# A decoder layer on one core: FFN weights staged earlier, gate blocks in single PSUM banks, two low halves moved to GpSimd

## The chip, the cores and the metric

The kernel runs on one core of a Trainium2 chip. Its time is device microseconds (us). Before the change it took 1652.49 us, the median of three runs (1648.84 to 1655.51). The profiled execution, from which all rows below come, took 1650.32 us; its span, from the first to the last instruction, is 1648.2 us. Engines: PE is TensorE (PEld its weight loads), DVE VectorE, ACT ScalarE, POOL GpSimd, SP SyncE; SPq, DVEq and so on are their queues.

## What is computed

One decoder layer on x of 1024 tokens by 1024 channels, in float32. The change touches its FFN only:

```python
    for i in range(DEPTH):
        h = rms_norm(x, g_mix[i])
        ...
        x = x + merged @ w_out[i]
        hf = rms_norm(x, g_ffn[i])
        x = x + (jax.nn.silu(hf @ w_ffn_gate[i]) * (hf @ w_ffn_up[i])) @ w_ffn_down[i]
        hp = rms_norm(x, g_ple[i])
        x = x + jax.nn.sigmoid(hp @ w_ple_gate[i]) * (p[i] @ w_ple_proj[i])
```

D_FF is 2816, so the gate and the up matrix have 22 blocks of 128 columns each.

## The kernel before

**Numbers and products.** Activations lie transposed, 128 channels by 1024 tokens per tile; a half of the tokens (512) is a column of PSUM work. Every float32 operand is split into a high and a low part (`split_w`, `split_x`: ACT copies the high part, L143 and L178; DVE or POOL subtracts, L144 and L179, to get the low part), and `gemm` (L181) adds three matmuls per piece of 128: high by high, high by low, low by high.

**Weights.** `want` writes a plan of all weights in the order of their use; `load(n)` issues the DMAs of the first n of the plan into two `raw` buffers, `stage(n)` splits the first n of the plan into high and low tiles, and `weights(name, i)` (L164) hands out the next one: it stages up to two ahead of the running number `weights.at`, loads three ahead, and then counts `weights.at` up. Both lists only grow, so `stage(n)` with an n below what is staged already does nothing.

**The FFN's front.** Inside a stretch whose order is the program's own (`tc.manual_schedule()`), eight blocks of w_out add into x (`out_block`), then the first two gate and up blocks, f = 0 and 1 (`FIRST`), are computed as plain products by `gate_up` (L1109), four calls: blocks 0 and 1 on the first half of the tokens, then blocks 0 and 1 on the second half. A call makes the gate product into PSUM, applies Silu on ACT (L1123) into a tile `sil`, makes the up product into PSUM, multiplies on DVE (L1127), and stores the hidden block. The list `between` holds work put into a call: after five eighths of the gate product, after the Silu, and after the multiplication. In the first call these are the statistics of the second half's norm (`nf[1].stats(1)`: a column sum on PE, L212, a scale on DVE, L203, and a power on POOL, L205) and the norm of that half (`later_half`: L1064 on DVE, then a split of each of eight units). The weights of block 1 are kept in tiles named `wk`, since both halves use them.

**PSUM.** Products go to `PG` tiles (two banks, two buffers) or `PM` tiles (one bank, three buffers); the column sums and the norms' replicated scales are `PM` tiles. An instruction that fills a buffer waits for the readers of what stood in it.

**Strassen pairs.** The other 20 gate and up blocks go in pairs through one level of Strassen's scheme (`strassen`, L1165): seven products of sums of weights (`pair_make`, from two raw tiles) and sums of activations (`sum_units`, L1073: DVE forms a sum, L1080, ACT its high half, DVE or POOL its low half, L179). The first pair's products run in the order 2, 4, 5, 3, 1, 6, 7; products 2 and 5 share one `PG` tile, 4 and 3 another; `six_seven(0)` and `six_seven(2)` make the eight sums for products 6 and 7 between products 4 and 5 and between 5 and 3. After them come the second pair's `pair_make` and its products. Outside the manual stretches a list scheduler sets the order.

**Into the down product.** A second manual stretch holds the last pair's products, the reload of the first hidden blocks (`hidden_load`, tiles `hd`, `fah`, `fal`), and `down` (L1277), whose weights `w_fd` come next in the plan. Ahead of the last pair's products stand two calls, `stage(1)` and `load(2)`.

Of the kernel before, what the change touches and what calls it, by code (L numbers as in the profile page):

```python
# [56 lines left out]
FIRST = (0, 1)  # L57
# [14 lines left out]
def tile_layer(ctx: ExitStack, tc: tile.TileContext, A, out):  # L72
    nc = tc.nc
    pe, dve, act, pool, sp = nc.tensor, nc.vector, nc.scalar, nc.gpsimd, nc.sync
# [10 lines left out]
    def nm(s):  # L85
        cnt[0] += 1
        return f"{s}_{cnt[0]}"

    def U(name="u", dt=F32, shape=(P, S)):
        return up.tile(list(shape), dt, tag="u", name=nm(name))  # L90
# [9 lines left out]
    def PG():  # L100
        return gp.tile([P, S], F32, tag="g", name=nm("g"))

    def PM(shape=(P, 512)):
        return mp.tile(list(shape), F32, tag="m", name=nm("m"))
# [14 lines left out]
    def pump(gen, k=1):  # L119
        for _ in range(k):  # L120
            next(gen, None)
# [12 lines left out]
    def load_w(src):  # L134
        n = src.shape[-1]
        raw = UW("raw", F32)[:, :n]
        sp.dma_start(raw, src)
        return raw

    def split_w(raw, lo_eng, keep):  # L140
        n = raw.shape[-1]
        hi, lo = (U("wk", FR), U("wk", FR)) if keep else (UW("whi")[:, :n], UW("wlo")[:, :n])
        act.activation(hi, raw, AF.Copy)  # L143
        lo_eng.tensor_tensor(lo, raw, hi.bitcast(F32), op=ALU.subtract)  # L144
        return hi, lo
# [8 lines left out]
    def load(n):  # L154
        while len(loaded) < min(n, len(plan)):
            n_, i_ = plan[len(loaded)][:2]
            loaded.append(load_w(A[n_] if i_ is None else A[n_][i_]))

    def stage(n):
        while len(made) < min(n, len(plan)):  # L160
            load(len(made) + 1)
            made.append(split_w(loaded[len(made)], *plan[len(made)][2:]))

    def weights(name, i=None, ahead=2):  # L164

        at_ = weights.at
        assert plan[at_][:2] == (name, i), (plan[at_], name, i)
        stage(at_ + ahead)
        load(at_ + ahead + 1)
        weights.at += 1  # L170
        t = made[at_]
        made[at_] = None
        return t
# [7 lines left out]
    def gemm(groups, W, X, k0=0, k1=None, fill=None, per=()):  # L181


        K = len(W)
        for k in range(k0, K if k1 is None else k1):
            if fill is not None:
                pump(fill, per[k])
            for t, (wi, xi) in enumerate(((0, 0), (0, 1), (1, 0))):
                for ps, sl in groups:
                    pe.matmul(ps, lhsT=W[k][wi], rhs=X[k][xi][:, sl],  # L190
                              start=(k == 0 and t == 0), stop=(k == K - 1 and t == 2))
# [4 lines left out]
    def wk(wt, K, off=0, width=P, stride=P):  # L196
        return [(wt[0][:, off + k * stride: off + k * stride + width],
                 wt[1][:, off + k * stride: off + k * stride + width]) for k in range(K)]
# [75 lines left out]
    xs = []  # L274
# [726 lines left out]
    for n2 in range(4):  # L1001
        wt = weights("w_ao", n2)
        for i in range(2):
# [4 lines left out]
            ps = PG()  # L1008
# [33 lines left out]
    XS, B12, B21 = {}, [], []  # L1042
# [4 lines left out]
    def x_unit(dst, a, lo_eng=None):  # L1047

        u = U("xc", FR)
        split_x(*parts(u), a, lo_eng)  # L1050
        dst.append(parts(u))

    def xs(i):
        return XS.setdefault(i, [])

    def norm_half(hf, r):

        sl = HV[hf]
        rep = replicate(r, 4)[0]
        yield  # L1060
        for k in range(9):
            if k < 8:
                h = x2[k][:, sl]
                dve.scalar_tensor_tensor(h, h, vec(V_FFN + k), rep, op0=ALU.mult, op1=ALU.mult)  # L1064
            if k:
                x_unit((B12 if k < 5 else xs(5)) if hf else (xs(2) if k < 5 else B21), x2[k - 1][:, sl])
            yield
# [5 lines left out]
    def sum_units(*iks, lo_eng=None):  # L1073
        todo = []
        for j, (i, k) in enumerate(iks):
            (p, u), op, (q, v) = SUMS[i]
            if j % 2 == 0:
                t = U("xsum")
            a = t[:, HV[j % 2]]
            dve.tensor_tensor(a, x2[p + k][:, HV[u]], x2[q + k][:, HV[v]], op=op)  # L1080
            todo.append((xs(i), a))
        for dst, a in todo:
            x_unit(dst, a, lo_eng)

    nf = [Norm(V_FFN) for _ in range(2)]

    def out_block(n, hf, before=None):
        wt = weights("w_out", n)
        pump(before or iter(()), 2)
        ps = PG()  # L1090
        gemm([(ps[:, 0:512], HV[hf])], wk(wt, 8), mT)
        dve.tensor_tensor(x2[n][:, HV[hf]], x2[n][:, HV[hf]], ps[:, 0:512], op=ALU.add)
        nf[hf].square(n, HV[hf])
        sp.dma_start(spill_x[n][:, HV[hf]], x2[n][:, HV[hf]])
# [7 lines left out]
    def hidden(f, s, sl):  # L1102
        if f not in spill_h:
            spill_h[f] = dp.tile([P, S], F32, tag=f"hd{f}", name=nm("hd"))
        sp.dma_start(spill_h[f][:, sl], s[:, sl])
# [3 lines left out]
    def gate_up(f, s, hf, X, between=()):  # L1109


        sl, half = HV[hf], slice(0, 512)
        between = [b or (lambda: None) for b in between] + [lambda: None] * (3 - len(between))
        for name in ("w_fg", "w_fu"):
            if (name, f) not in firsts:
                firsts[name, f] = weights(name, f)
            wt = firsts[name, f]
            ps = PG()
            if name == "w_fg":
                gemm([(ps[:, half], half)], wk(wt, 8), X, 0, 5)  # L1120
                between[0]()
                gemm([(ps[:, half], half)], wk(wt, 8), X, 5)
                act.activation(s[:, sl], ps[:, half], AF.Silu)  # L1123
                between[1]()
            else:
                gemm([(ps[:, half], half)], wk(wt, 8), X)
                dve.tensor_tensor(s[:, sl], s[:, sl], ps[:, half], op=ALU.mult)  # L1127
                hidden(f, s, sl)
                between[2]()
# [3 lines left out]
    def pair_load(m):  # L1133

        name, i = m
        ra, rb = UW("raw", F32), UW("raw", F32)
        for t, c, j in ((ra, 0, 0), (ra, 1, 1), (rb, 0, 1), (rb, 1, 0)):
            sp.dma_start(t[:, HV[c]], A[name][i + c][:, HV[j]])
        raws[m] = ra, rb
# [79 lines left out]
    with tc.manual_schedule():  # L1219
        nh = None  # L1220
        for n in range(8):
            out_block(n, 1, nh)
            if n == 0:
                nf[0].stats(0)
            if n == 1:
                nh = norm_half(0, nf[0].r)
                pump(nh)
        pump(nh, 9)
        hs = [U("sil") for _ in FIRST]
        one_of = lambda i, lo_eng=None: lambda: sum_units(*((i, k) for k in range(4)), lo_eng=lo_eng)  # L1230

        def later_half():
            pump(norm_half(1, nf[1].r), 99)

        def pair0():
            pair_load(ms[0])
            one_of(4, pool)()

        def pair1():
            pair_load(ms[1])  # L1240

        def six_seven(k):
            return lambda: (sum_units((6, k), (7, k)), sum_units((6, k + 1)), sum_units((7, k + 1), lo_eng=pool))

        gate_up(FIRST[0], hs[0], 0, xs(2) + B21, (lambda: nf[1].stats(1), later_half))
        gate_up(FIRST[1], hs[1], 0, xs(2) + B21, (None, None, pair0))
        gate_up(FIRST[0], hs[0], 1, B12 + xs(5), (None, one_of(3), lambda: pair_make(ms[0])))
        gate_up(FIRST[1], hs[1], 1, B12 + xs(5), (None, one_of(1), pair1))
        gated(ms[0], strassen(ms[0], {4: six_seven(0), 5: six_seven(2), 1: lambda: pair_make(ms[1], pool)}))
# [5 lines left out]
    def hidden_load(ci, fs=None):  # L1255
        for f in fs or CHUNKS[ci]:
            h, hi, lo = U("hd"), U("fah", FR), U("fal", FR)
            sp.dma_start(h, spill_h[f])
            split_x(hi, lo, h)
            aa.setdefault(ci, []).append((hi, lo))  # L1260
# [34 lines left out]
    with tc.manual_schedule():  # L1295
        def back(*fs):
            return lambda: hidden_load(0, fs)

        stage(1)
        load(2)  # L1300
        rr = strassen(ms[-1], {4: back(*CHUNKS[0][:2]), 5: back(*CHUNKS[0][2:])})
        for n in range(2):
            x2_load(n)
        gated(ms[-1], rr)
        for ci in range(len(CHUNKS) - 1):
            nxt = load_next(ci, (2, 3, 5, 6))
            for n in down(ci, (0, 1), nxt):
                if ci == 0 and n < 6:
                    x2_load(n + 2)
# [14 lines left out]
    for hf in range(2):  # L1324
        sl = HV[hf]
        for n in range(8):
# [3 lines left out]
            ps, s, o = PG(), U("psig"), U("o")  # L1330
# [79 lines left out]
```

## Time and profile before

| | |
|---|---|
| median of three runs | 1652.49 us (1648.84 to 1655.51) |
| profiled execution: time, span | 1650.32 us, 1648.2 us |
| PE, DVE, ACT, POOL busy, share of the span | 97%, 69%, 43%, 9% |
| mean granted TensorE clock | 0.987 of full speed |
| chain that ended last | PE 51%, DVE 3%, ACT 1% of the span in merged steps |
| hand-over w_out to FFN, first blocks | about 854 to 935 us of the span |
| last pair to down product | about 1267 to 1316 us of the span |

How to read it: PE works nearly without a break, so what counts is each stretch in which it stands still, what ended that stretch, and how fast its next matmuls go. Busy time of other engines counts where PE waits for them. In a timeline a row is a run of like instructions: start, length, engine, line, operation, tiles, count, and in brackets the engine's idle time before it and what ended that.

### The profile page before, as it was taken

How to read it: one execution, taken by the hardware profiler on the slowest of the kernel's cores; microseconds unless marked ns; L12 is line 12 of the kernel's file. 1: busy time of each engine (PE TensorE's matmuls, PEld its weight loads, DVE VectorE, ACT ScalarE, POOL GpSimd, SP SyncE). 2: the span in 40 equal slices, each digit the busy share in tenths (PEclk: the TensorE clock that was granted, in tenths of full speed). 3: DMA queues.
4: the chain of work that ended last, by engine and by line, in shares of the span. 5: the costliest groups of instructions: out<-in, count | busy, mean ns of one | idle time of the engine just before them, and what ended most of it. 6: DMA issues, size and time to landing. Idle time of an engine off the chain costs nothing.

```text
span 1648.2 us, 20331 instructions
## 1 busy us (share of the span) xinstructions
PE 1592.8 (97%) x7736; PEld 1328.4 (81%) x7736; DVE 1139.4 (69%) x1806; ACT 714.5 (43%) x1066; POOL 147.0 (9%) x134
## 2 busy tenths in 40 slices
PE   7999999999999999999998899999999799999998
PEld 5888888888878888878886678888888688888887
DVE  4669999884899777656476766777766444446763
ACT  5456475868733677633243332232233222113441
POOL 2100100000202421320001100000000000000210
PEclk9999999999999999999999999999999899999999
DMA  7430122222222854246441122222221542223263
GB/s 264 115 90 27 64 89 90 91 101 77 98 82 94 213 154 109 97 176 246 146 136 45 58 90 90 77 77 77 102 92 63 184 148 102 103 83 108 84 205 134
DMA packets 61538, 184.69 MB, mean 112 GB/s; under 512 B 7296, under 2 KB 7808, under 8 KB 61440
## 3 DMA queue, kind: packets, MB, share of 16 engines
q1 hardware_dynamic: 61440, 183.38, 32.9%
q8 instruction: 61, 1.00, 0.3%
q14 instruction: 37, 0.30, 0.1%
HBM read 134.60 MB, written 45.09 MB: 109 GB/s over the span
## 4 chain that ended last, share of the span: by engine, by line
PE 51%; DVE 3%; ACT 1%; issue 0%; DMA 0%; SPq 0%; ACTq 0%; DVEq 0%
PE g L190 41%; PE m L190 9%; DVE xsum L1080 1%; DVE xc L179 1%; DMA raw<-w_fd 0%; DVE x L1064 0%; ACT xc L178 0%; DVE wlo L179 0%; PE m L212 0%; PE f L190 0%; DVE h L248 0%; DVE raw L1157 0%; DVE c L1215 0%; ACT whi L178 0%; DVE sil L1127 0%
## 5 line engine op out<-in xcount | busy, mean ns | idle before, releaser
L143 ACT ACTIVATE whi<-raw 128x1024 fp32r<-128x1024 f32 x110 | 115.5, 1052 | 219.9 <-PE g L190 185.1
L190 PE MATMUL g<-hhi,whi 128*128 128x512 f32 (+2 forms) x656 | 200.9, 387 | 2.1 <-ACT vt L658 1.5
L190 PE MATMUL g<-hlo,whi 128*128 128x512 f32 (+2 forms) x656 | 199.4, 385 | 2.6 <-POOL hlo L179 1.3
L190 PE MATMUL g<-hhi,wlo 128*128 128x512 f32 (+2 forms) x656 | 199.4, 385 | 0.0
L144 DVE TENSOR_TENSOR wlo<-raw,whi 128x1024 fp32r<-128x1024 f32 x102 | 127.3, 1250 | 52.1 <-ACT whi L143 51.9
L613 DVE SCALAR_TENSOR_TENSOR cacc<-glu,vecs,cacc 128x994 f32<-128x994 f32 (+14 forms) x120 | 151.8, 1265 | 2.7 <-ACT cacc L610 1.9
L511 ACT ACTIVATE junka<-Y,tr 128x1024 bf16<-128x1024 f32 (+3 forms) x128 | 126.3, 987 | 46.0 <-DVE tr L536 23.2
L190 PEld LDWEIGHTS g<-hlo,whi 128*128 128x128 f32 (+1 forms) x656 | 122.1, 187 | 27.9 <-POOL hlo L179 2.1
L190 PEld LDWEIGHTS g<-hhi,whi 128*128 128x128 f32 (+1 forms) x656 | 121.6, 187 | 25.6 <-ACT vt L658 1.9
L190 PEld LDWEIGHTS g<-hhi,wlo 128*128 128x128 f32 (+1 forms) x656 | 122.1, 187 | 24.2
L1288 DVE TENSOR_TENSOR x<-x,g 128x1024 f32<-128x1024 f32 (+1 forms) x56 | 59.8, 1067 | 114.8 <-PE g L190 114.8
L205 POOL TENSOR_TENSOR r<-ms,mhalf 128x16 f32<-128x16 f32 (+2 forms) x14 | 34.8, 2489 | 1045.9 <-DVE ms L203 1030.3
L190 PE MATMUL g<-fah,whi 128*128 128x512 f32 x352 | 115.3, 394 | 9.8 <-ACT whi L143 9.4
L190 PE MATMUL g<-xc,whi 128*128 128x512 f32 x384 | 119.9, 393 | 4.7 <-DVE sil L1127 3.3
L190 PE MATMUL g<-fal,whi 128*128 128x512 f32 x352 | 114.5, 392 | 0.0
L190 PE MATMUL g<-fah,wlo 128*128 128x512 f32 x352 | 114.4, 392 | 0.0
L190 PE MATMUL g<-xc,w 128*128 128x512 f32 x480 | 112.0, 389 | 1.1 <-ACT w L178 1.1
L190 PEld LDWEIGHTS g<-xc,w 128*128 128x128 f32 x480 | 90.0, 188 | 20.2 <-ACT w L178 1.5
L190 PE MATMUL m<-xc,whi 128*128 128x512 f32 x320 | 99.1, 390 | 0.8 <-ACT xc L178 0.6
L190 PEld LDWEIGHTS g<-xc,whi 128*128 128x128 f32 x384 | 72.5, 190 | 20.7 <-DVE sil L1127 3.7
L190 PEld LDWEIGHTS g<-fah,whi 128*128 128x128 f32 x352 | 66.8, 190 | 24.7 <-ACT whi L143 9.9
L190 PEld LDWEIGHTS g<-fah,wlo 128*128 128x128 f32 x352 | 66.6, 189 | 14.1
(238 smaller groups left out, 3197.3 us busy)
## 6 DMA issues: line engine op xcount, KB each, us to landing
raw<-w_fd SPq DMA_DIRECT2D x26, 512.0 KB, 3.5
hd<-hd SPq DMA_DIRECT2D x22, 512.0 KB, 4.5
raw<-w_fg SPq DMA_DIRECT2D x40, 256.0 KB, 2.8
raw<-w_fu SPq DMA_DIRECT2D x40, 256.0 KB, 2.8
hd<-c SPq DMA_DIRECT2D x20, 512.0 KB, 2.8
x<-xT SPq DMA_DIRECT2D x16, 512.0 KB, 9.3
sgd<-sg SPq DMA_DIRECT2D x16, 512.0 KB, 2.9
raw<-w_out SPq DMA_DIRECT2D x16, 512.0 KB, 3.7
```

Of the source, the lines that this page charges most:

```text
L143: act.activation(hi, raw, AF.Copy)
L144: lo_eng.tensor_tensor(lo, raw, hi.bitcast(F32), op=ALU.subtract)
L179: (lo_eng or dve).tensor_tensor(lo, x, hi.bitcast(F32), op=ALU.subtract)
L190: pe.matmul(ps, lhsT=W[k][wi], rhs=X[k][xi][:, sl], start=(k == 0 and t == 0), stop=(k == K - 1 and t == 2))
L205: pool.tensor_tensor(r, ms, mhalf[:, :width], op=ALU.pow)
L511: act.activation(junka[:, :n], ysl(b), AF.Sign, scale=-1.0, bias=self.tr[:, c], accum_out=self.cn[:, c])
L613: dve.scalar_tensor_tensor(acc[:, sl], g, w, acc[:, sl], op0=ALU.mult, op1=ALU.add)
L1080: dve.tensor_tensor(a, x2[p + k][:, HV[u]], x2[q + k][:, HV[v]], op=op)
L1288: dve.tensor_tensor(x2[n][:, sl], x2[n][:, sl], ps[:, sl], op=ALU.add)
```

## The change

`gate_up` takes a `PM` tile for the gate product and keeps a `PG` tile for the up product. A function `first_stats` replaces the bare statistics in the first call and stages three ahead of the running number behind them. `six_seven` pairs the sums of one product in a tile instead of one sum of each, and gives both low halves of product 7 to POOL. `stage(1)` and `load(2)` become calls by the running number.

```diff
-            ps = PG()
+            ps = PM() if name == "w_fg" else PG()
...
+        def first_stats():
+            nf[1].stats(1)
+            stage(weights.at + 3)
+
...
         def six_seven(k):
-            return lambda: (sum_units((6, k), (7, k)), sum_units((6, k + 1)), sum_units((7, k + 1), lo_eng=pool))
-
-        gate_up(FIRST[0], hs[0], 0, xs(2) + B21, (lambda: nf[1].stats(1), later_half))
+            return lambda: (sum_units((6, k), (6, k + 1)), sum_units((7, k), (7, k + 1), lo_eng=pool))
+
+        gate_up(FIRST[0], hs[0], 0, xs(2) + B21, (first_stats, later_half))
...
-        stage(1)
-        load(2)
+        stage(weights.at + 1)
+        load(weights.at + 2)
         rr = strassen(ms[-1], {4: back(*CHUNKS[0][:2]), 5: back(*CHUNKS[0][2:])})
```

On ACT, at the first `gate_up` call, the order was (whi is the up weight of block 0, wk the two weights of block 1, xc the units of the second half's norm):

```order
L143 ACTIVATE whi_7779<-raw_7745 128x1024
L1123 ACT_TABLE_LOAD
L1123 ACTIVATE sil_7777<-g_7785 128x512
L178 ACTIVATE xc_7827<-x_1238_7131 128x512
...
L178 ACTIVATE xc_7854<-x_1252_7152 128x512
L143 ACTIVATE wk_7857<-raw_7783 128x1024
L143 ACTIVATE wk_7891<-raw_7861 128x1024
L1123 ACTIVATE sil_7778<-g_7895 128x512
```

and is now:

```order
L143 ACTIVATE whi_7779<-raw_7745 128x1024
L143 ACTIVATE wk_7810<-raw_7783 128x1024
L143 ACTIVATE wk_7816<-raw_7814 128x1024
L1123 ACT_TABLE_LOAD
L1123 ACTIVATE sil_7777<-m_7785 128x512
L178 ACTIVATE xc_7837<-x_1238_7131 128x512
...
L178 ACTIVATE xc_7864<-x_1252_7152 128x512
L1123 ACTIVATE sil_7778<-m_7895 128x512
```

The two `wk` copies moved from behind the norm's eight units to ahead of the first Silu; on DVE their low halves moved in the same way, from behind the eight units to right behind the statistics.

On SP, ahead of the last pair's products, the order was (raw from w_fd is the down product's weight, hd the reloaded hidden blocks and the stored ones):

```order
L1105 DMA hd_10551<-c_1736_10314 128x1024
L1258 DMA hd_10713<-hd_7889 128x1024
...
L1264 DMA x_1801_10810<-x2d_7136 128x1024
L1105 DMA hd_10813<-c_1774_10578 128x1024
L1105 DMA hd_10816<-c_1773_10577 128x1024
L137 DMA raw_10818<-w_fd 128x1024
L137 DMA raw_10824<-w_fd 128x1024
```

and is now:

```order
L1105 DMA hd_10549<-c_1734_10312 128x1024
L137 DMA raw_10680<-w_fd 128x1024
L137 DMA raw_10686<-w_fd 128x1024
L1262 DMA hd_10719<-hd_7893 128x1024
...
L1268 DMA x_1803_10816<-x2d_7136 128x1024
L1105 DMA hd_10819<-c_1772_10576 128x1024
L1105 DMA hd_10822<-c_1771_10575 128x1024
```

Two loads of w_fd moved ahead of four reloads of hidden blocks, two of x and two stores. The first one's high half now stands on ACT between the last weight copy of the last pair (L178) and the copy of product 5 of the pair before (L1185); its low half on DVE ahead of L1188.

On DVE, in the sums for products 6 and 7, the first half of the order was:

```order
L1182 TENSOR_TENSOR c_1410_8143<-s_1408_8141,g_8145 128x512
L1080 TENSOR_TENSOR xsum_8172<-x_1238_7131 128x512
L1080 TENSOR_TENSOR xsum_8172<-x_1246_7143 128x512
L179 TENSOR_TENSOR xc_8175<-xsum_8172,xc_8175 128x512
L179 TENSOR_TENSOR xc_8178<-xsum_8172,xc_8178 128x512
L1080 TENSOR_TENSOR xsum_8181<-x_1240_7134 128x512
L179 TENSOR_TENSOR xc_8183<-xsum_8181,xc_8183 128x512
L1080 TENSOR_TENSOR xsum_8186<-x_1248_7146 128x512
```

and is now:

```order
L1182 TENSOR_TENSOR c_1410_8143<-s_1408_8141,g_8145 128x512
L1080 TENSOR_TENSOR xsum_8172<-x_1238_7131 128x512
L1080 TENSOR_TENSOR xsum_8172<-x_1240_7134 128x512
L179 TENSOR_TENSOR xc_8175<-xsum_8172,xc_8175 128x512
L179 TENSOR_TENSOR xc_8178<-xsum_8172,xc_8178 128x512
L1080 TENSOR_TENSOR xsum_8181<-x_1246_7143 128x512
L1080 TENSOR_TENSOR xsum_8181<-x_1248_7146 128x512
```

One of three low halves left DVE, and the same in the second call; POOL has four in place of two. PE's order is the same but for the PSUM tiles' names.

## Rows read from the trace of the kernel before

**Rows 1.** The page's first part: busy time of each engine, its share of the span and its instructions.

```profile
PE 1592.8 (97%) x7736; PEld 1328.4 (81%) x7736; DVE 1139.4 (69%) x1806; ACT 714.5 (43%) x1066; POOL 147.0 (9%) x134
```

**Rows 2.** Who waited for whom, PE alone, over the whole span: what it waited for, us in total, times, the longest in us.

```profile
PE g L190 <- ACT whi L143: 9.4, 1, 9.4
...
PE g L190 <- ACT wk L143: 5.3, 1, 5.3
PE g L190 <- DVE sil L1127: 3.3, 1, 3.3
...
PE m L190 <- ACT one L178: 2.7, 1, 2.7
...
PE g L190 <- ACT w L178: 1.1, 1, 1.1
```

**Rows 3.** Busy time by stretch: us, then busy us and count of PE, PEld, DVE, ACT and POOL, the granted TensorE clock as a share of full speed, the DMA share and GB/s.

```profile
871.70:876.00 4.30, 4.24 (x11) 2.91 (x12) 2.96 (x3) 0.92 (x1) 0.00 (x0) 0.58 0.16 61
...
912.50:916.50 4.00, 3.98 (x10) 3.12 (x11) 0.00 (x0) 0.00 (x0) 0.00 (x0) 0.57 0.70 205
...
1309.80:1315.80 6.00, 5.93 (x14) 4.66 (x15) 2.45 (x2) 1.07 (x2) 0.00 (x0) 0.52 0.56 206
1316.00:1328.00 12.00, 12.00 (x54) 9.89 (x54) 4.71 (x4) 4.01 (x4) 0.00 (x0) 1.00 0.60 243
```

**Rows 4.** PE's timeline: the products of block 1 on the first half and on the second half of the tokens, and the first matmuls of the down product.

```profile
871.73 13.05 PE L190 MATMUL g<-xc,wk 128*128 128x512 f32 x48 [5.31 <-ACT wk L143]
...
895.49 11.04 PE L190 MATMUL g<-xc,wk 128*128 128x512 f32 x48
...
1309.87 1.22 PE L190 MATMUL g<-fah,whi 128*128 128x512 f32 x2 [9.44 <-ACT whi L143]
```

**Rows 5.** The timelines of ACT, DVE and SP in the FFN's front, 853 to 885 us.

```profile
860.53 0.60 ACT L1123 ACTIVATE sil<-g 128x512 f32<-128x512 f32 x1 [2.78 <-PE g L190]
...
870.63 1.99 ACT L143 ACTIVATE wk<-raw 128x1024 fp32r<-128x1024 f32 x2
...
860.97 1.41 DVE L1064 SCALAR_TENSOR_TENSOR x<-x,vecs,m 128x512 f32<-128x512 f32 x2 [2.48 <-PE m L222]
...
869.99 1.47 DVE L179 TENSOR_TENSOR xc<-x,xc 128x512 fp32r<-128x512 f32 x2
...
884.88 0.69 DVE L1127 TENSOR_TENSOR sil<-sil,g 128x512 f32<-128x512 f32 x1 [10.21 <-PE g L190]
...
855.27 0.38 SPq L137 DMA_DIRECT2D raw<-w_fg  x1
857.73 0.33 SPq L137 DMA_DIRECT2D raw<-w_fu  x1
```

**Rows 6.** DMA issues of whole weight blocks: count, KB each, median us from issue to landing; and the smallest, median and largest time to landing of the four w_fd loads between 1265 and 1325 us.

```profile
raw<-w_fg SPq DMA_DIRECT2D x2, 512.0 KB, 3.4
raw<-w_fu SPq DMA_DIRECT2D x2, 512.0 KB, 3.9
...
DMA to landing us min/median/max: 3.6/5.3/7.9
```

**Rows 7.** The timelines of SP, DVE and ACT from the pair before the last to the down product, 1267 to 1312 us.

```profile
1278.17 9.02 SPq L1258 DMA_DIRECT2D hd<-hd  x4
...
1303.83 7.60 SPq L137 DMA_DIRECT2D raw<-w_fd  x3
...
1269.34 1.23 DVE L1157 TENSOR_TENSOR raw<-raw,raw 128x1024 f32<-128x1024 f32 x1
...
1276.91 1.23 DVE L179 TENSOR_TENSOR wlo<-wd,whi 128x1024 fp32r<-128x1024 f32 x1 [3.35 <-ACT whi L178]
1281.50 0.69 DVE L1188 TENSOR_TENSOR c<-g,s 128x512 f32<-128x512 f32 x1 [3.36 <-PE g L190]
...
1278.71 0.60 ACT L1185 ACTIVATE s<-g 128x512 f32<-128x512 f32 x1 [1.83 <-PE g L190]
```

**Rows 8.** The timelines of DVE and POOL with the sums of activations, 884 to 938 us.

```profile
885.48 9.29 DVE L1080 TENSOR_TENSOR xsum<-x,x 128x512 f32<-128x512 f32 x8
...
906.97 2.49 DVE L1080 TENSOR_TENSOR xsum<-x,x 128x512 f32<-128x512 f32 x4
...
917.84 1.29 DVE L1080 TENSOR_TENSOR xsum<-x 128x512 f32<-128x512 f32 x2
...
921.82 0.69 DVE L179 TENSOR_TENSOR xc<-xsum,xc 128x512 fp32r<-128x512 f32 x1 [0.70 <-ACT xc L178]
...
924.88 1.75 DVE L179 TENSOR_TENSOR xc<-xsum,xc 128x512 fp32r<-128x512 f32 x2 [0.56 <-ACT xc L178]
...
927.92 0.69 DVE L179 TENSOR_TENSOR xc<-xsum,xc 128x512 fp32r<-128x512 f32 x1 [0.70 <-ACT xc L178]
...
929.14 0.68 DVE L1188 TENSOR_TENSOR c<-g,s 128x512 f32<-128x512 f32 x1
...
931.53 0.68 DVE L1195 TENSOR_TENSOR c<-c,m 128x512 f32<-128x512 f32 x1
932.12 2.00 DVE L1153 TENSOR_TENSOR wd<-raw 128x512 f32<-128x512 f32 x1
...
886.91 6.71 POOL L179 TENSOR_TENSOR xc<-xsum,xc 128x512 fp32r<-128x512 f32 x4 [27.34 <-ACT xc L178]
...
931.22 2.36 POOL L179 TENSOR_TENSOR w<-raw,w 128x1024 fp32r<-128x1024 f32 x1
```

## The prediction, written before the changed kernel was run

> **What bounds the kernel now.** I read the page's first part first: PE is busy 97% of the span [rows 1], so time can be taken only where PE stands still or runs slowly. The list of PE's waits comes next [rows 2]. Two are long and single: 9.4 us for a weight copy of L143 and 5.3 us for another (tile wk). Behind them stand 3.3 us for the multiplication of L1127, 2.7 us for the tile `one` of a pair's weights, and 1.1 us for another copy of such weights. The timelines place them: the wk wait ends at 871.73, in the FFN's front; the 9.44 us end at 1309.87, at the first matmul of the down product [rows 4]. The windows show what follows a stop: a granted clock of 0.58 of full speed behind the first, 0.57 behind the 3.3 us, 0.52 behind the longest, which is in the main the lower level of 1.2 GHz, and 1.00 from 1316 us on [rows 3]. So a stop costs its own length and a slow stretch behind it.
>
> **Part 1: the front.** The first matmuls of block 1 waited because ACT copied its weights (wk) at 870.63, behind the eight units of the second half's norm, although their DMAs had been issued at 855.27 and 857.73 [rows 5]. Whole blocks of these two matrices landed after 3.4 and 3.9 us [rows 6], so at 858.7 and 861.6. In the new order ACT copies them then: two copies in 1.99 us by the row at 870.63 [rows 5], so about 1.0 each, the second done at 862.7; DVE subtracts until about 864.0. PE wants the first at 866.4 (871.73 less 5.31) and the second one product later. The wait of 5.3 goes. The slow stretch behind it goes too: the 48 matmuls of block 1 took 13.05 us there and 11.04 us on the second half [rows 4], a difference of 2.0.
>
> What it pushes back: the Silu at 860.53 and the norm, which DVE began at 860.97 [rows 5], now begin behind the two low halves, at about 864.0, 3.0 us later. The norm's last low half, done at 869.99 + 1.47 = 871.5 [rows 5], is done at 874.5. PE, which no longer stops, comes to the second half at 866.4 + 11.0 = 877.4. The cover is 2.9 us for the last unit, and more, since PE uses that unit last. Were both loads to take 7.9 us, the longest in the rows [rows 6], the last wk low half would be done at about 868.0 and the norm 7.0 late, at 878.5; PE asks for the last unit 21 matmuls of 0.23 us into the block, at 882.2. Still nothing is lost. Everything behind moves as one: DVE had stood idle 10.21 us for block 1's up product before 884.88 [rows 5], so its following work starts as much earlier as PE does. The 3.3 us for L1127 therefore stay: DVE's work from 884.88 to that multiplication keeps its length, and so does PE's. **Term: 5.3 + 2.0 = 7.3 us gained; bounds 5.3 (the slow stretch turns up elsewhere) and 8.9.** The upper end is this: behind the 3.3 us stop ten matmuls took 4.0 us [rows 3] where ten of 0.23 take 2.3, and whether a stop of that length brings the clock down may differ from run to run.
>
> **Part 2: into the down product.** Before, the first w_fd load was issued at 1303.83, behind the last pair's stores, and PE stood 9.44 us [rows 4, 7]. `stage(1)` and `load(2)` did nothing. Now the load stands ahead of the reloads. Its buffer is free when L1157 has read it, at 1269.34 + 1.23 = 1270.6 [rows 7]; with a landing of 3.6 to 7.9 us [rows 6] it is there at 1274.2 to 1278.5. The copy's target tile is free when product 5 of the pair before has ended, which is also what L1185 waited for at 1278.71 [rows 7]. So ACT copies from about 1278.7 to 1279.8 and L1185 follows 1.1 us late, at 1279.8 to 1280.4; DVE subtracts 1279.8 to 1281.0. L1188, next on DVE, waited for PE until 1281.50 anyway [rows 7]: cover 0.5 us. L1185 releases the PSUM tile of the last pair's first product, which PE begins behind 1281.5: cover 1.1 us. SP is free for the reloads of hidden blocks, issued from 1278.17 [rows 7], since the other buffer's last reader on DVE stands ahead of the row at 1276.91 and the second w_fd load has gone by then. So w_fd is split some 19 us before PE wants it at 1300.4. The blocks of the down product behind the first one get their weights earlier than before too, and PE had no further stop there. **Term: 9.4 for the stop and 2.8 for the slow 14 matmuls behind it (6.0 us [rows 3] against 14 x 0.23 = 3.2): 12.2 us; bounds 9.4 and 12.2.**
>
> **Part 3: gate blocks in single banks.** No instruction is added. What it changes is whose reading frees a tile: the last pair of gate blocks used to hand its two-bank tile to product 2 after a Silu; now product 2 waits for an earlier up block's L1127. Product 4 still takes the tile of the last up block, hence still waits for its L1127. **Term: 0**, hidden by readers that end several us earlier; if that cover went, the 3.3 us stop would grow by what the reader is late.
>
> **Part 4: the sums for products 6 and 7.** DVE's chain from 917.84 to 929.14 (11.3 us) holds eight sums and six low halves, with waits of 0.70, 0.56 and 0.70 us for ACT [rows 8]. Four sums without POOL work beside them took 2.49 us [rows 8], so an operation takes about 0.61. Taking two away saves 1.2, and forming two sums in a row lets ACT work ahead, which may save the 2.0 of waits. Against it stands POOL: eight sums beside four POOL halves (6.71 us) took 9.29 us instead of 8 x 0.61 = 4.9, so one POOL half cost DVE 1.1 us; and L1153, otherwise 0.68, took 2.00 beside a POOL operation of 2.36. L1195, which reads PSUM, kept 0.68 in the same stretch [rows 8]. The Trainium skill ("SBUF — State Buffer", section "SBUF: two separate sides") says that DVE operations with two SBUF inputs and GpSimd operations exclude each other for a whole instruction. The trace agrees where a POOL half meets such sums; by that rule over all four halves Part 4 is at its lower bound below and the sum is 17.7 us, by the rows as I place them 20.0. In the new order two POOL halves meet the second call's sums (2.2 us lost) and two fall beside DVE's PSUM reads. The chain: 12 x 0.61 + 2.2 + about 0.7 of waiting = 10.2, 1.1 us earlier. But POOL then comes to its weight half (2.36) behind two more halves, and L1153 waits for it as before: from about 928 on, 2 x 1.3 + 2.4 ends at 933.0, where it ended at 933.6. `one`, for which PE waited 2.7, follows L1153. **Term: 0.5 gained; bounds 4.0 gained (all waits and no POOL cost: 7.3 instead of 11.3) and 1.8 lost (four POOL halves in the way: 7.3 + 4.4 + 1.4 = 13.1).** I take the value near the middle because the rows at 886.91 and 931.22 are the same operations on the same engines.
>
> **The sum.** 7.3 + 12.2 + 0 + 0.5 = 20.0 us from the profiled execution's 1650.3: 1630.3. The median of the runs is 2.2 above that execution; I put the change's median halfway, at **1631.4**.
>
> **Rivals.**
> - *POOL blocks DVE throughout*, the rule named in Part 4. Part 4 at its lower end: 1.8 lost instead of 0.5 gained, so 1631.4 + 2.3 = 1633.7. For it: 9.29 us at 885.48 [rows 8]. Against it: only half of the moved work stands beside two-input sums.
> - *The front's gain is given back at L1127.* If DVE's chain to that multiplication is set by something other than PE, such as a pair's weights landing, PE waits 7.3 us more there: 1638.7. Against it: DVE's 10.21 us idle ended by PE [rows 5].
> - *The down product finds another late input* (hidden blocks or a PSUM tile), and Part 2 yields nothing: 1643.6. Against it: the one wait listed there is the weight copy [rows 2].
> - *The staged copy blocks ACT: slower.* The copy now stands ahead of L1185. From a landing of about 1280 on, L1185 and with it PE's last pair is late by the same amount. If the load were held until 1303.83 as before, with a landing at 1308.8, PE would stop at 1281.7 (the end of its matmuls ahead of L1188's row) until about 1310.5: 28.8 us in place of 9.4, so 1631.4 + 28.8 + 2.8 (the slow stretch stays) = 1663.0. It is slower than before once the stop passes 1652.5 - 1631.4 - 2.8 = 18.3 us, that is, from a landing of about 1298 on. For it: SP's queue is in order. Against it: the buffer is free at 1270.6 [rows 7] and nothing late stands ahead.
> - *It doesn't do what it says*: the staging calls change nothing, 1652. The instruction order speaks against it.
> - *The 3.3 us stop goes too*, with its slow 1.7: 1626.4.
>
> **How the numbers follow.** Chances: forecast 0.66; POOL 0.16; front given back 0.07; down 0.05; slower 0.02; nothing done 0.02; more gained 0.02. A measurement of this kernel tells about 0.5% (8.3 us) from no change. All but three cases are faster by more; the down case, at 8.9 us, lies on the bound and is shared out. So faster 0.94, same 0.04, slower 0.02. The range reaches from 1625.5 (the last rival, less a us) to 1640.0 (the front given back, plus a us); the largest part of it is the spread of the runs shown (1648.84 to 1655.51) and Part 4's bounds.
>
> **What would show it.** PE without the 5.3 and 9.4 us waits; clock 1.00 in the two stretches behind them; the wk copies ahead of the first Silu, done near 863 on ACT; w_fd issued near 1270, less 7, and split some 20 us before PE uses it; the 3.3 us wait for L1127 still there; `one` late by some 2 to 3 us; four POOL halves of 1.3 to 1.7 us with stretched DVE sums beside them. A new PE wait over 2 us in the first stretch of the down product, or DVE taking longer for the sums than the 11.3 us from 917.84 to 929.14, would make it wrong.

## The result, and the profile after

The changed kernel took 1628.23 us, the median of five runs (1627.05 to 1632.04); five runs of the kernel before, the three shown ahead of the prediction among them, had a median of 1649.86. The ratio is 0.9868 [0.985, 0.9886]. The forecast was 1631.4, in a range of 1625.5 to 1640.0. The profiled execution of after took 1629.16 us, its span 1627.3.

The page's first part: busy time of each engine, share of the span, instructions.

```profile
PE 1590.6 (98%) x7736; PEld 1329.4 (82%) x7736; DVE 1140.8 (70%) x1804; ACT 714.2 (44%) x1066; POOL 150.1 (9%) x136
```

PE's busy time is 2.2 us less than in [rows 1], of 21 us in all; so most came out of time in which it stood still. PE's waits (us in total, times, longest):

```profile
PE g L190 <- ACT phi L178: 5.6, 3, 4.6
...
PE g L190 <- DVE sil L1127: 3.3, 1, 3.3
PE m L190 <- ACT one L178: 2.9, 1, 2.9
```

The 9.4 and the 5.3 us of [rows 2] are gone; the 3.3 us for L1127 and the wait for `one` stand nearly as they did (2.9 for 2.7). The 1.1 us for `w` are gone from the list too; the 12 matmuls ahead of it took 4.66 us instead of 3.29. PE's timeline, and one row of DVE's, give the ledger:

```profile
865.96 0.39 PE L190 MATMUL g<-xc,wlo 128*128 128x512 f32 x1
866.18 5.60 PE L190 MATMUL m<-xc,wk 128*128 128x512 f32 x24
871.62 5.60 PE L190 MATMUL g<-xc,wk 128*128 128x512 f32 x24
877.06 0.62 PE L190 MATMUL m<-xc,whi 128*128 128x512 f32 x2
...
904.97 0.73 PE L190 MATMUL g<-xc,whi 128*128 128x512 f32 x2 [3.26 <-DVE sil L1127]
...
914.90 2.88 PE L190 MATMUL m<-xc,one 128*128 128x512 f32 x12
...
926.30 4.66 PE L190 MATMUL m<-xc,one 128*128 128x512 f32 x12 [2.85 <-ACT one L178]
...
1283.55 2.88 PE L190 MATMUL m<-xc,one 128*128 128x512 f32 x12
...
1291.71 0.62 PE L190 MATMUL g<-fah,whi 128*128 128x512 f32 x2
...
1302.79 1.22 DVE L1292 TENSOR_TENSOR x<-x,g 128x1024 f32<-128x1024 f32 x1 [4.22 <-PE g L190]
```

The rows of before that answer to them, besides [rows 4]:

```profile
866.03 0.39 PE L190 MATMUL g<-xc,wlo 128*128 128x512 f32 x1
...
884.61 0.62 PE L190 MATMUL g<-xc,whi 128*128 128x512 f32 x2
...
922.41 2.88 PE L190 MATMUL m<-xc,one 128*128 128x512 f32 x12
...
934.89 3.29 PE L190 MATMUL m<-xc,one 128*128 128x512 f32 x12 [2.74 <-ACT one L178]
...
1292.11 2.88 PE L190 MATMUL m<-xc,one 128*128 128x512 f32 x12
...
1323.78 1.22 DVE L1288 TENSOR_TENSOR x<-x,g 128x1024 f32<-128x1024 f32 x1 [4.22 <-PE g L190]
```

| start on PE of | before | after | earlier by | since the line above |
|---|---|---|---|---|
| the last matmul ahead of block 1 | 866.03 | 865.96 | 0.07 | 0.07, ahead of the change |
| block 0, second half of the tokens | 884.61 | 877.06 | 7.55 | 7.5: the front |
| the first pair's product 1 (first tile `one`) | 922.41 | 914.90 | 7.51 | 0.0: the stop for L1127 kept its place |
| the second pair's product 1 | 934.89 | 926.30 | 8.59 | 1.1: the sums |
| the last pair's product 1 | 1292.11 | 1283.55 | 8.56 | 0.0 |
| the down product | 1309.87 | 1291.71 | 18.16 | 9.6: the stop |
| the down product's second add (on DVE, L1288, now L1292) | 1323.78 | 1302.79 | 20.99 | 2.8: the slow stretch behind it |

The windows that answer to [rows 3] (us; busy us and count of PE, PEld, DVE, ACT, POOL; granted clock; DMA share; GB/s):

```profile
871.70:876.00 4.30, 4.30 (x21) 3.56 (x20) 2.94 (x5) 1.57 (x3) 0.00 (x0) 1.00 0.08 31
904.97:908.97 4.00, 4.00 (x12) 3.14 (x13) 0.00 (x0) 0.00 (x0) 0.00 (x0) 0.64 0.69 203
1292.00:1298.00 6.00, 6.00 (x28) 4.99 (x27) 4.66 (x5) 0.00 (x0) 0.00 (x0) 1.00 0.59 203
```

The clock is 1.00 where it was 0.58 and 0.52, and still low behind the stop that stayed: 12 matmuls there in 4 us, 28 in 6 us in the down product.

ACT's timeline in the front, and SP's and ACT's into the down product (start, length, engine, line):

```profile
858.76 1.06 ACT L143 ACTIVATE wk<-raw 128x1024 fp32r<-128x1024 f32 x1 [2.39 <-DMA raw<-w_fg]
861.42 1.06 ACT L143 ACTIVATE wk<-raw 128x1024 fp32r<-128x1024 f32 x1 [1.60 <-DMA raw<-w_fu]
...
1262.07 2.70 SPq L137 DMA_DIRECT2D raw<-w_fd  x2
1269.61 9.02 SPq L1262 DMA_DIRECT2D hd<-hd  x4
...
1269.92 1.06 ACT L143 ACTIVATE whi<-raw 128x1024 fp32r<-128x1024 f32 x1 [1.60 <-PE g L190]
1270.89 0.58 ACT L1185 ACTIVATE s<-g 128x512 f32<-128x512 f32 x1
```

The wk copies begin at 858.76 and 861.42, as their loads land; in [rows 5] they stood at 870.63. The loads of w_fd go at 1262.07, where [rows 7] had 1303.83, ahead of the reloads. The copy at 1269.92 waited for PE and not for its DMA, and ends 20.7 us before PE wants it.

DVE's and POOL's timelines with the sums, which answer to [rows 8]:

```profile
877.94 9.29 DVE L1080 TENSOR_TENSOR xsum<-x,x 128x512 f32<-128x512 f32 x8
...
910.22 1.29 DVE L1080 TENSOR_TENSOR xsum<-x 128x512 f32<-128x512 f32 x2
...
912.82 3.59 DVE L1080 TENSOR_TENSOR xsum<-x 128x512 f32<-128x512 f32 x4
916.33 2.38 DVE L179 TENSOR_TENSOR xc<-xsum,xc 128x512 fp32r<-128x512 f32 x2
918.63 1.28 DVE L1080 TENSOR_TENSOR xsum<-x 128x512 f32<-128x512 f32 x2
919.84 0.68 DVE L1188 TENSOR_TENSOR c<-g,s 128x512 f32<-128x512 f32 x1
...
922.83 2.70 DVE L1153 TENSOR_TENSOR wd<-raw 128x512 f32<-128x512 f32 x1
...
914.25 3.31 POOL L179 TENSOR_TENSOR xc<-xsum,xc 128x512 fp32r<-128x512 f32 x2 [28.17 <-ACT xc L178]
920.12 2.54 POOL L179 TENSOR_TENSOR xc<-xsum,xc 128x512 fp32r<-128x512 f32 x2 [2.56 <-ACT xc L178]
922.62 2.36 POOL L179 TENSOR_TENSOR w<-raw,w 128x1024 fp32r<-128x1024 f32 x1
```

DVE's chain from the first sum to L1188 takes 9.6 us (910.22 to 919.84), where it took 11.3. Two POOL halves lie on it: four sums take 3.59 us instead of 2.49, two low halves 2.38 instead of 1.29, 1.1 us for each POOL half. The other two fall beside L1188 and its followers, which read PSUM and keep 0.68 us. Then the weight half holds L1153 up: 2.70 us, in before 2.00, where alone it takes 0.68.

### The profile page after: what moved, and what is told of

Its sections match the earlier page's. It is cut to its first block, busy times and chain, and to the rows that moved or that the text cites. A ratio compares the mean times of both kernels' runs of the same rounds, so it can differ in the third digit from the quotient of the medians.

```text
span 1627.3 us, 20334 instructions
## 1 busy us (share of the span) xinstructions
PE 1590.6 (98%) x7736; PEld 1329.4 (82%) x7736; DVE 1140.8 (70%) x1804; ACT 714.2 (44%) x1066; POOL 150.1 (9%) x136
## 4 chain that ended last, share of the span: by engine, by line
PE 52%; DVE 3%; ACT 0%; issue 0%; ACTq 0%; DVEq 0%
PE g L190 41%; PE m L190 10%; DVE xsum L1080 1%; DVE xc L179 0%; DVE wlo L179 0%; DVE wd L1153 0%; PE m L212 0%; DVE h L248 0%; PE f L190 0%; ACT whi L178 0%; DVE sil L1127 0%; PE m L222 0%; ACT one L178 0%; DVE raw L1157 0%; DVE sal L1010 0%
## 5 line engine op out<-in xcount | busy, mean ns | idle before, releaser
L1292 DVE TENSOR_TENSOR x<-x,g 128x1024 f32<-128x1024 f32 (+1 forms) x56 | 59.8, 1067 | 107.7 <-PE g L190 107.7
L190 PE MATMUL g<-xc,whi 128*128 128x512 f32 x352 | 109.9, 394 | 4.7 <-DVE sil L1127 3.3
L190 PE MATMUL m<-xc,whi 128*128 128x512 f32 x352 | 108.9, 390 | 0.0
L190 PEld LDWEIGHTS g<-xc,whi 128*128 128x128 f32 x352 | 66.7, 190 | 19.5 <-DVE sil L1127 3.7
L814 DVE SCALAR_TENSOR_TENSOR pt<-m,pt 128x512 f16<-128x512 f32 (+3 forms) x96 | 50.6, 554 | 38.9 <-ACT pt L813 38.4
```

What stands on the lines that cost most here:

```text
L190: pe.matmul(ps, lhsT=W[k][wi], rhs=X[k][xi][:, sl], start=(k == 0 and t == 0), stop=(k == K - 1 and t == 2))
L814: dve.scalar_tensor_tensor(lo[:, c0:c0 + cw], pt[:, :cw], PSCALE, hi[:, c0:c0 + cw], op0=ALU.mult, op1=ALU.subtract)
L1292: dve.tensor_tensor(x2[n][:, sl], x2[n][:, sl], ps[:, sl], op=ALU.add)
```

## The experiments

Kernels e1 to e4 are the kernel before with one part of the change each; e5 and e9 cut and join parts; e6 to e8, e10b and e10 are the changed kernel with edits. Differences in us are between medians; the ratio's 95% interval tells how sure they are.

**e1_down**, the kernel before with:

```diff
-        stage(1)
-        load(2)
+        stage(weights.at + 1)
+        load(weights.at + 2)
```

> Only the staging of w_fd by the running number, ahead of the last pair. Theory (the stop at the down product and the slow matmuls behind it are one piece by itself): PE's 9.4 us wait for the copy of L143 is gone, the first down matmul comes 9.6 us earlier against the last pair and the next blocks 12.4 us earlier; all other PE waits stay (5.3 wk, 3.3 L1127, 2.7 one). 12.4 us faster than before, about 0.75%. Rival (the parts help each other): under 9 us or over 15.

1637.22 us against 1649.81: ratio 0.9923 [0.9908, 0.9938], 12.6 us. The 9.4 us wait is gone, the FFN's other waits keep their lengths. Part 2 stands alone at its forecast size.

**e5_load**, the kernel before with the load early and the split where it was:

```diff
-        stage(1)
-        load(2)
+        load(weights.at + 2)
```

> The kernel before with load(2) replaced by load(weights.at + 2) ahead of the last pair's products, and no early split: the two w_fd loads go early, their splits stay in the down product's first call. Theory A (the stop was the landing): ACT copies the weight right behind its last hidden block, at about 1292, DVE subtracts behind L1215, at 1304.6 in the clock of the kernel before, and PE stops about 3 to 4 us for the low half instead of 9.4; 6 to 9 us faster. Theory B (the stop was the split, wherever the data is): PE's stop stays over 8 us and the time within 2 us of before.

1641.78 against 1649.11: 0.9951 [0.9934, 0.9968], 7.3 us. PE's timeline at the down product:

```profile
1299.40 0.62 PE L190 MATMUL g<-fah,whi 128*128 128x512 f32 x2
1303.75 0.73 PE L190 MATMUL g<-fah,wlo 128*128 128x512 f32 x2 [3.28 <-DVE wlo L144]
```

The stop of 9.4 us is now one of 3.3, four matmuls further on, ended by DVE: the low half stands behind L1215, which combines the last pair (2.35 us from 1300.20). So the late landing made most of the stop, and the call that splits early is worth the rest, by the medians 5.3 us (12.6 less 7.3).

**e2_front**, the kernel before with the staging in the first call alone:

```diff
+        def first_stats():
+            nf[1].stats(1)
+            stage(weights.at + 3)
...
-        gate_up(FIRST[0], hs[0], 0, xs(2) + B21, (lambda: nf[1].stats(1), later_half))
+        gate_up(FIRST[0], hs[0], 0, xs(2) + B21, (first_stats, later_half))
```

> Only first_stats (block 1's weights staged ahead of the norm), with two-bank tiles for the gate blocks as before. Theory A, formed after the result: the gate and the up products share two two-bank tiles, so block 1's up product takes the tile of block 0's up product, whose reader L1127 stands on DVE behind the norm and ends at about 874.8 us; PE wants the tile at 871.6, so it stops there for 3.2 us, and the gain is 7.5 - 3.2 = 4.3 us or, with a slow stretch, 3. Theory B (the prediction's term of 0 for the single banks holds everywhere): no such stop and 7.5 us faster.

1646.2 against 1649.81: 0.9982 [0.9972, 0.9991], only 3.6 us. The 5.3 us stop went and a new one came. ACT's and PE's timelines:

```profile
865.18 5.60 PE L190 MATMUL g<-xc,wk 128*128 128x512 f32 x24
873.02 5.73 PE L190 MATMUL g<-xc,wk 128*128 128x512 f32 x24 [2.24 <-ACT sil L1123]
...
872.39 0.58 ACT L1123 ACTIVATE sil<-g 128x512 f32<-128x512 f32 x1
```

Block 1's up product began 0.05 us after the Silu of its own gate product had ended (872.97): it takes a two-bank tile that this Silu reads. The Silu stands behind the norm's eight copies on ACT, and the staging had put those back. Theory A was right that a reader is late; I had named L1127 and 3.2 us, it was L1123 and 2.24. The stop for L1127 came as before, with a slow stretch 1.1 us longer than in after.

**e3_banks**, the kernel before with the single banks alone:

```diff
-            ps = PG()
+            ps = PM() if name == "w_fg" else PG()
```

> Only the gate blocks in one-bank tiles. Both theories: no PE wait is removed, the 5.3, 9.4, 3.3 and 2.7 us waits stay within 0.2 us, time as before within 0.3%.

1650.29: 1.0009 [0.9996, 1.0023], every wait of the FFN as before within 0.1 us. **e9_front_banks** joins e2's edit and this one.

> first_stats and the one-bank gate tiles together, nothing else. Theory A (the banks let the front's staging pay in full: alone, block 1's up product waited 2.2 us for the Silu that stands behind the norm's copies on ACT): no PE wait for L1123 in the front, block 0's second half starts 7.5 us earlier than before, 7.5 us faster. Theory B (the banks are worth nothing): as the front alone, 3.6 us faster.

1642.12 against 1649.11: 0.9951 [0.9936, 0.9966], 7.0 us; block 1's two products run without a break (869.21 and 874.65), and no wait for L1123 is listed. So 3.6 with the first, nothing that the times can tell with the second, 7.0 with both.

**e4_sums**, the kernel before with the new pairing and POOL's two halves:

```diff
-            return lambda: (sum_units((6, k), (7, k)), sum_units((6, k + 1)), sum_units((7, k + 1), lo_eng=pool))
+            return lambda: (sum_units((6, k), (6, k + 1)), sum_units((7, k), (7, k + 1), lo_eng=pool))
```

> Only the regrouped sums with four low halves of product 7 on POOL. Theory (POOL halves beside DVE's sums cost 1.1 us each, two of four meet them; grouping removes the waits for ACT): DVE's chain of sums takes 9.6 us instead of 11.3, and the second pair's product 1 starts 1.1 us earlier against product 1 of the first; 1 us faster, not to be told apart in the time. Rival (the lock costs more than the regrouping saves): the chain takes 12 us or more and product 1 starts later than before.

1649.02: 0.9993 [0.9978, 1.0008]; no difference that the times can tell. In the trace DVE's chain is 9.6 us (921.65 to 931.27), and the two pairs' products 1 stand 11.51 us apart, where they stood 12.48: 1.0 us, in after 1.1.

```profile
926.24 2.88 PE L190 MATMUL m<-xc,one 128*128 128x512 f32 x12
...
937.75 4.52 PE L190 MATMUL m<-xc,one 128*128 128x512 f32 x12 [2.85 <-ACT one L178]
```

**e6_sums_dve**, the changed kernel with all four of product 7's low halves on DVE:

```diff
-            return lambda: (sum_units((6, k), (6, k + 1)), sum_units((7, k), (7, k + 1), lo_eng=pool))
+            return lambda: (sum_units((6, k), (6, k + 1)), sum_units((7, k), (7, k + 1)))
```

> The changed kernel with the four low halves of product 7 on DVE. Theory A (a POOL half beside DVE's two-input sums costs DVE 1.1 us, more than the 0.6 us it takes off DVE): DVE's chain of sums takes 9.7 to 10.3 us although it holds four operations more (9.6 now), POOL comes to its weight half 0.8 us earlier, L1153 ends and the second pair's product 1 starts 0.8 us earlier; time as the changed kernel, 1627 to 1629. Theory B (POOL takes the work off DVE at no cost): the chain is 2.4 us longer, 12.0, and that product starts 2 us later.

1626.93, 0.986 [0.9843, 0.9877] of before. DVE's chain takes 10.5 us for 16 operations, 0.9 more than in after for four operations more; L1153 takes 0.68 instead of 2.70, and the second product 1 comes 10.10 us after the first, 1.3 sooner than in after. PE then waits 1.16 us for a weight copy (ACT w), but the 12 matmuls ahead of that take 3.29 us instead of 4.66:

```profile
924.85 3.29 PE L190 MATMUL m<-xc,one 128*128 128x512 f32 x12 [1.77 <-ACT one L178]
```

So the next product still comes 1.35 us sooner after the first product 1 (14.55 for 15.90). Product 7's four halves on POOL thus cost 1.3 us more in this trace than they saved, by L1153; the times can't tell. So Part 4's gain is the pairing's, with POOL against it. The two halves that the change moved were not tried apart from the two that POOL had before.

**e7_four_dve**, the changed kernel with an older pair of POOL's halves, in `pair0`, taken back:

```diff
-            one_of(4, pool)()
+            one_of(4)()
```

> The changed kernel with the four low halves of the sums for product 4 on DVE, where POOL's four took 6.71 us beside eight sums that took 9.29. Theory A (the lock): the eight sums take 4.9 us and the eight halves 4.9, so L1127 comes 2.0 us earlier and PE's wait for it falls from 3.3 to about 1.3 us; 2 to 3.7 us faster than the changed kernel. Theory B: DVE has 2.4 us more work ahead of L1127 and the wait grows to 5.7 us; 2 to 4 us slower.

1624.17, 0.9847 [0.9829, 0.9865] of before, by the medians some 4 us faster than after. DVE's timeline:

```profile
876.24 2.49 DVE L1080 TENSOR_TENSOR xsum<-x,x 128x512 f32<-128x512 f32 x4
878.65 2.49 DVE L179 TENSOR_TENSOR xc<-xsum,xc 128x512 fp32r<-128x512 f32 x4
881.06 2.49 DVE L1080 TENSOR_TENSOR xsum<-x,x 128x512 f32<-128x512 f32 x4
883.47 2.49 DVE L179 TENSOR_TENSOR xc<-xsum,xc 128x512 fp32r<-128x512 f32 x4
```

The eight sums that took 9.29 us beside POOL take 4.98 without it. With the four halves now its own, DVE is still 1.8 us quicker. PE's stop for L1127 shrinks from 3.26 to 1.86 us, and the matmuls behind it run at full clock: product 1 comes 8.29 us behind the stop, in after 9.93. That is 3.0 us in the trace, 1.4 of stop and 1.6 of clock.

The changed kernel was run once more beside the kernels that follow (**after_again**: 1627.72, 0.9869 [0.9854, 0.9884]).

> The changed kernel once more, beside the three variants on the same chip: 1628 us, PE stopping 3.3 us for L1127 and 2.9 us for one, as in its first profile. If the slow stretch behind the 3.3 us stop differs by over 1 us, its length is chance from run to run and no variant's gain of that size is shown by a single profile.

Both waits came back (3.26 and 2.85 us), and product 1 came 9.93 us behind the stop, to the hundredth as in the first profile. Yet that slow stretch doesn't always come. e9's program is the same as after's up to there, and its trace has the same stop without it:

```profile
907.99 0.73 PE L190 MATMUL g<-xc,whi 128*128 128x512 f32 x2 [3.26 <-DVE sil L1127]
...
916.29 2.88 PE L190 MATMUL m<-xc,one 128*128 128x512 f32 x12
```

Product 1 comes 8.30 us behind the stop, as in e7. So of e7's gain the 1.4 us of the stop are shown to be the edit's; the 1.6 us of clock count only in executions in which the clock falls behind the longer stop.

**e8_no_pool**, e6 and e7 and:

```diff
-... 1: lambda: pair_make(ms[1], pool)}))
+... 1: lambda: pair_make(ms[1])}))
```

> The changed kernel with every low half of this stretch on DVE: those of one_of(4), of product 7, and of the second pair's pair_make. Theory A (POOL's halves cost DVE 1.1 us each when they meet its sums): the 4.0 us of the four DVE halves in one_of(4) stay gained, product 7's stay neutral, and pair_make's low halves on DVE put back 2.5 us or more that POOL had taken off it ahead of product 1: 1.5 to 4 us faster than the changed kernel, so behind the version that leaves the weight half with POOL. Theory B (no work on POOL ever pays here): 4 us faster or more.

1624.78, 2.9 us below after_again. `one` is waited for 3.2 us, since DVE's weight half (1.22 us) stands ahead of L1153. Theory A: taking POOL's other halves away gains nothing over e7.

**e10b_later**, the changed kernel with the work between the last gate and up product moved behind L1127:

```diff
         def pair1():
             pair_load(ms[1])
+            one_of(1)()
...
-        gate_up(FIRST[1], hs[1], 1, B12 + xs(5), (None, one_of(1), pair1))
+        gate_up(FIRST[1], hs[1], 1, B12 + xs(5), (None, None, pair1))
```

> The changed kernel with only one_of(1) moved behind the last L1127; POOL keeps its halves. Theory A: the 3.3 us stop and its slow 1.7 us are gone, 4 to 5 us faster than the changed kernel. Theory B: the work moved is late for the product that reads it, time within 2 us of the changed kernel.

1628.12 in the median, 1623.0 to 1629.72: by the times it is inconclusive. In its trace the stop for L1127 is gone, and from block 1's last up product (895.69) to product 1 (912.01) it takes 16.32 us, in after 21.52, 1.6 of the difference being the slow stretch; some 0.5 is lost behind that. But this execution reached block 1 at 868.49, where after_again did at 863.02, the most of it in a stretch that the edit doesn't touch (last section).

**e10_best**, e6, e7 and e10b together (POOL's halves that it takes back are four of the first kind and four of product 7, where the expectation says eight and two):

> The changed kernel with three further edits: the eight low halves that follow the second half's norm are DVE's and not POOL's, product 7's two low halves likewise, and the work called one_of(1) (eight more sums with their halves) is done behind the last plain gate block's multiplication L1127 instead of ahead of it. Theory A (DVE's queue ahead of L1127 is what makes PE's 3.3 us stop, and POOL's halves lengthen that queue): the stop for L1127 is gone (3.3 us), the slow stretch behind it too (about 1.7 us), the tile one comes up to 1.3 us earlier: 5 to 6.3 us faster than the changed kernel. Theory B (the eight sums moved behind L1127 are only late elsewhere): product 1 or product 5 waits for its xc by what was moved, up to 4.9 us, and the time is within 2 us of the changed kernel's.

1621.79 us, 0.9839 [0.9823, 0.9856] of before, 5.9 us under after_again on the same chip, and the lowest median of all; e7's interval overlaps this one. PE's list of waits begins now:

```profile
PE g L190 <- ACT phi L178: 6.2, 3, 5.1
PE g L787 <- DMA kst<-kdh: 3.5, 1, 3.5
PE m L190 <- ACT one L178: 2.1, 1, 2.1
```

The first is the program's start, the second in the attention; of the FFN's only `one` is left. From block 1's last up product to the second pair's product 2 it takes 31.17 us (891.23 to 922.40), in after_again 37.47 (890.22 to 927.69); from there to the down product 360.93 and 360.91. So the trace has 6.3 us, all in that stretch, and theory A's sum, with the slow stretch in it.

## Why the prediction was right, point by point

**Part 1, the front: right in size, incomplete in its working.** 7.3 us were forecast; the ledger has 7.5. The stop was taken as the 5.31 us of idle time, which count from the end of the matmul before (866.42); matmuls in a row start 0.23 us apart and take 0.39, so the next one would have started at 866.26. The 3.3 us for L1127 stayed, as argued from DVE's idle time. What the working missed is e2: it counted the norm's last unit among the late work and found it covered, and not block 1's Silu behind it on ACT, which releases a PSUM tile.

**Part 3, the banks: the term of 0 was wrong as an independent term.** It is 0 in the old order (e3) and takes away a 2.24 us stop in the new one (e2 against e9, 3.6 and 7.0 us). The prediction said that the cover for whose reading frees a tile was several us, from a trace in which block 1 still came 5.3 us late. The sum came out right because the change carries both edits; the working hadn't seen that it needs both, and in that much the number was luck.

**Part 2, the down product: right.** 12.2 forecast, 9.6 + 2.8 = 12.4 in the ledger (the stop again 0.16 more than its idle time), 12.6 by e1. The issue was foreseen near 1263 and came at 1262.07, and the copy waited for PE's tile as argued. The copy ahead of L1185 cost PE nothing: the last pair's product 1 is 8.56 us early, as that of the pair before it (1259.07 for 1267.63). The rival in which the copy blocks ACT fell there.

**Part 4, the sums: right in kind, too small.** 0.5 forecast, 1.1 measured (1.0 in e4). The price of 1.1 us for a POOL half that meets such sums was right, twice, and L1153 was held up as foreseen. The step that failed is the 0.7 us of waiting for ACT left in the chain of 10.2: with two sums in a row ACT keeps ahead, and 12 x 0.61 + 2.2 = 9.5 is nearly what DVE took, 9.6. The Trainium skill ("SBUF — State Buffer", section "SBUF: two separate sides") has DVE operations with two SBUF inputs and GpSimd's exclude each other; the traces agree (9.29 us in after, 4.98 in e7, for the same eight sums). The rival that charged it to all four halves, 1633.7, fell, because two of them met PSUM reads, which keep 0.68 us.

**The other rivals.** L1127 didn't take the front's gain back (3.26 us as before). No late input stood behind w_fd. The 3.3 us stop needed its own edits (e7, e10). That a stop of that length may or may not bring the clock down, as Part 1 says of its upper bound, e9 shows.

**The size.** The forecast of 1631.4 is 3.2 us over the median. Of that 1.1 is the half step from the profiled execution towards the median of the three runs shown, which five runs put at 1649.86, below that execution; 0.8 are Parts 4 and 2, and 0.2 Part 1 and what lies ahead of the change; 0.2 lie outside the ledger; the last 0.9 is the difference of after's median from its profiled execution.

## What to carry to other kernels

Two edits that are worth nothing and little alone may be worth their sum only together: where a stop is taken out, ask again who releases each buffer, by the times that will hold then. A piece given to a second engine was not free here where both engines read the same memory: price the operations that it will stand beside, and put it beside those that read PSUM. A call that compares a count with a list that has grown past it does nothing; write it relative to the running number, and issue the load and the split early, since by the medians each was about half of that part's gain. And a slow stretch behind a stop, read from a single trace, is worth a look at the other traces before it is counted as gained.

## What the runs showed of the hardware that was not expected

The granted clock behind a stop is no fixed function of its length. Ten traces have the stop for L1127 at 3.26 or 3.27 us. In nine of them the granted clock fell behind it, and product 1 came 9.88 to 11.03 us after the stop; in e9 it stayed at 1.00 over the next four us, with 18 matmuls where after has 12, and product 1 came after 8.30 us. At 1.86 and 1.87 us (e7, e8) and behind e2's 2.24 us the next matmuls show no slow stretch; but behind stops for `one` of 2.07 us (e10) and 2.74 us (before) the next 12 matmuls took 4.54 and 3.29 us. In the layer's attention, which no edit touches, PE stops for a tile `kst`, 3.68 us in after and 3.50 in after_again, and the windows behind, first of after and then of after_again, read:

```profile
540.00:550.00 10.00, 6.32 (x22) 4.73 (x22) 5.37 (x10) 3.31 (x4) 7.72 (x3) 0.71 1.04 314
550.00:560.00 10.00, 10.00 (x48) 9.53 (x47) 4.44 (x11) 4.58 (x7) 5.24 (x2) 0.60 0.36 86
```

```profile
540.00:550.00 10.00, 6.50 (x28) 4.85 (x28) 5.73 (x10) 3.48 (x4) 7.29 (x3) 0.83 1.02 315
550.00:560.00 10.00, 10.00 (x85) 9.37 (x85) 7.88 (x22) 8.15 (x13) 5.26 (x2) 1.00 0.84 199
```

The same program at nearly the same stop: 48 matmuls in the second window at a clock of 0.60, and 85 at 1.00. From that stop's end to the first transpose of `attn` (L853) it is 38.03 us in after and 33.84 in after_again; e10b was like the first (38.40, a clock of 0.54 in the window), e10_best like the second (33.90, 1.00). Over all fourteen traces it is 33.8 to 34.3 us in eight, 38.0 to 38.4 in five and 35.4 in before; stops of 3.02 us (e4) and 3.00 us (e7) went different ways, 38.23 and 33.92. So 4.2 to 4.5 us come and go between executions of the same instructions, about as much as e10b had gained. It also stands in the ledger: at that stop's end after was 2.7 us ahead of before (545.30 for 548.02), and it lost nearly all of it there, so that the two came to the front within 0.07 us by chance. That it hides e10b's gain in the median fits its runs, 1623.0 to 1629.72, but their traces were not taken. What decides it is open; no run here tells.
